# One transformer-style block on one core: the order of modulation's loads, and where splits and waits stand in five places

## The chip, the cores and the metric

The kernel runs on one core of a Trainium2 chip. The metric is the device time of one execution in microseconds (us), as the median over runs. The core's engines work side by side, each through its own list of instructions in order: TensorE (PE; its weight loads are PEld), VectorE (DVE), ScalarE (ACT), GpSimd (POOL) and SyncE (SP), which here issues the DMA transfers.

## The reference

One layer over 1024 latent tokens and 256 context tokens, width 1024, in float32. Cut to its core:

```python
mod_x = silu(c) @ w_ada + b_ada            # six vectors of 1024: shift, scale, gate, twice
mod_c = silu(c_ctx) @ w_ada + b_ada        # the same for the context tokens
px = modulate(rms_norm(x, g_pre_mix), sh_m, sc_m) @ w_in
pc = modulate(rms_norm(ctx, g_pre_mix), csh_m, csc_m) @ w_in
att_x = window_attention(...)              # 8 query heads, 2 key heads, band of 128, context keys, a sink
ml_x = mlstm_output(mlstm_bidir(...))      # chunkwise mLSTM in both directions, 4 heads
mix_x = concatenate([att_x, ml_x]) @ w_out
x = x + gt_m * rms_norm(mix_x, g_post_mix)
h = modulate(rms_norm(x, g_pre_ffn), sh_f, sc_f)
fx = (silu(gate) * up) @ w_ffn_out         # gate, up = split(h @ w_ffn_in), hidden 2816
x = x + gt_f * rms_norm(fx, g_post_ffn)
```

modulate(h, shift, scale) is h * (1 + scale) + shift.

## The kernel before

**Splits.** To keep float32's accuracy on TensorE, an operand is split into a high part (a cast to a shorter format, on ACT, `split` at L60) and a low part (the operand less the high part, on DVE at L61, on GpSimd in a few places), and a product is three matmuls, high by high, low by high and high by low (`mm3`, L72 to L74). [...]

**The modulation** (L265 to L320). Two of the six sections of `w_ada` are needed ahead of the input projection: `sec` 1 (scale), then `sec` 0 (shift). Each is eight tiles `wa` of 128x1024 (512 KB, L272), for the rows kt 0 to 7. The table `PLAIN` says which tiles are multiplied unsplit (`pr<-wa,cz`); the others are split into `hh` and `hl`. The results of a section (`pr`, 4x1024) are copied into `Vc`, half by ACT (L302) and half by DVE (L303), then transposed into columns (`pcol`, L309), which become `scol` (scale) and `hcol` (shift). All of this runs while weights arrive. `last` and `issue_after` chain the transfers into one order on SP: a transfer is issued behind the one named. Two more transfers stand there: `const` (masks, selections and the 128x128 identity, tile `cst`) and `bcv` (tile `bcr`), and the two pieces of the gate weights `w1` (`wr`, L260), each split into `w1h` and `w1l`.

**The first slabs.** Each of the ten tiles of 128 tokens is normalised, transposed and modulated: `prep_a` (load, squares on ACT, square root, and the scaling by GpSimd at L198; `prep_a2` at L183 for tile 2), `prep_t` (transposes on TensorE, L210), `prep_m` (eviction with the scale, L224), `prep_b` (adding `hcol`, L235; high parts, L244 and L247; low parts, L248). Then `slab` multiplies a tile by columns of `w_in`.

**Attention items.** Sixteen items (n, g), a tile of queries and a key head each. `PLAN_ML` (the first eight, which also carry the mLSTM) and `PLAN` (the rest) are strings whose letters order an item's operations: A scores, T transposes of the probabilities (L917), M the products with the values, N the normalising of the next item, O the output, z, V, s, x the mLSTM, l loads. An item's softmax runs on ACT (L898) and DVE (L889) two items ahead, and GpSimd scales the probabilities (L903). `WLOADS` says at which item `wout_load(j)` is called for each of the eight row tiles of `w_out`: it loads the raw tile (512 KB), casts it on ACT (L858) and subtracts on GpSimd (L859).

**Output projection and FFN.** `omm(n, hf, ks)` are the matmuls of tile n with `w_out`, `opost1` and `opost2` the norm and the residual, `otr` the transposes for the FFN (L1132), `omod` their modulation. The functions' calls around the last attention items and the first FFN products are written out by hand. ACT loads a table of functions when it turns from exponentials to square roots (L177). In the FFN, `xv` are PSUM tiles of the input product, evicted by ACT (L1282) or DVE; `es_add(0)` is a DVE addition for the first of them. A call to `keep_in_program_order` holds an instruction at its place in the program on its engine; other instructions are ordered by a list scheduler.

Of the kernel before, what the change touches and what calls it, by code (L numbers as in the profile page):

```python
# [29 lines left out]
CID, CUP, CLO, CSEL, CIND = 0, 128, 256, 384, 512  # L30
NCONST = 576
VSIL, VCONV, VGML, VBADA, VGPM, VGPF = 0, 16, 28, 32, 64, 72
NVEC = 80
PLAN_ML = "T0 A0 A1 A2 A3 T1 T2 T3 M0 M1 T4 V0 N0 M2 M3 M4 O z V1 w s N1 x"
PLAN = "T0 A0 A1 A2 A3 T1 T2 T3 N0 M0 T4 M1 M2 N1 M3 M4 O z l"
PLAN13 = "T0 A0 A1 A2 A3 m T1 T2 P0 T3 N0 M0 T4 M1 P1 M2 N1 M3 P2 M4 O P3 l"
WLOADS = {8: (0, 1), 9: (2,), 10: (3,), 11: (4,), 12: (5, 6), 13: (7,)}


def body(tc, x, ctx, vecs, bcv, bada, gqm, gqf, wada, ws1, ws2, wt, wout, wfi, wfo,  # L40
# [65 lines left out]
    ident = cst[:, CID:CID + P]  # L106
# [73 lines left out]
    def prep_a2(i):  # L180
        r = st[:, 10 + i:11 + i]
        tc.keep_in_program_order(dve.reciprocal(r, r))
        pool.tensor_scalar(xts[i], xts[i], r, 1.0, MUL, MUL)  # L183

    def prep_a(i, parts=(0, 1)):

        j = i - NT
        xt = xts[i] = R(4 + i % 4, f"xt{i}", (D,))
        xd[i] = dma(xt, x[i * P:(i + 1) * P] if i < NT else ctx[j * P:(j + 1) * P])
        hraw[i] = R((2, 3)[i] if i < 2 else (12, 13, 8, 9, 10, 11)[i % 6], f"hraw{i}", (KT, P))  # L190
        sq = act.activation(hraw[i].rearrange("p a b -> p (a b)"), xt, AF.Square, accum_out=st[:, i:i + 1])
        if i > 1:
            tc.keep_in_program_order(sq)
        if 1 not in parts:
            act.activation(st[:, 10 + i:11 + i], st[:, i:i + 1], AF.Sqrt, bias=epst, scale=1.0 / D)
            return
        rms_r(st[:, 10 + i:11 + i], st[:, i:i + 1])
        pool.tensor_scalar(xt, xt, st[:, 10 + i:11 + i], 1.0, MUL, MUL)  # L198
# [18 lines left out]
    def prep_m(i):  # L217
# [5 lines left out]
        for b in range(2):  # L223
            dve.tensor_tensor(raw2[i][b], pts[i][b], hcast(scol[:, i // NT, 4 * b:4 * b + 4]), MUL)  # L224

    def prep_b(i):
# [7 lines left out]
        for b in (1, 0) if i == 0 else range(2):  # L234
            r = (dve if i < 2 else pool).tensor_tensor(raws_[b], raws_[b], hcast(hcol[:, q, 4 * b:4 * b + 4]), ADD)  # L235
            if i == 1:
                tc.keep_in_program_order(r)
        if i == 0:
            prep_a2(2)
        for b in range(2):  # L240
# [7 lines left out]
            dve.tensor_tensor(ls[b][:, :, tok], raws_[b], h_.bitcast(F32), SUB)  # L248
# [9 lines left out]
    def w1_load(i):  # L258
        w1r[i] = R(i, f"wr1_{i}", (4, 272))
        r = dma(w1r[i], ws1[:, i])  # L260
        for k in (0, 2):
            split(w1h[i][:, k:k + 2], w1l[i][:, k:k + 2], w1r[i][:, k:k + 2])
        return r.ins

    PLAIN = {1: (0, 2, 4), 0: (0, 3, 7)}  # L265
    last, nsp = None, 0
    for sec in (1, 0):
        pr = [pa.tile([4, 512], F32, name=f"pr{sec}{i}", tag="mm", bufs=4) for i in range(2)]
        for kt in range(KT):
# [10 lines left out]
            for n, (a, b) in enumerate(ops):  # L280
                for i in range(2):
                    pe.matmul(pr[i], a[:, kt, :], b[:, i * 512:(i + 1) * 512], start=kt == 0,
                              stop=kt == KT - 1 and n == len(ops) - 1)
            if (sec, kt) == (1, 0):
                with tc.issue_after(last):
                    dma(cst, const)
                    last = dma(bcr, bcast(bcv)).ins
                dve.tensor_scalar(mF, up, -1.0, -NEG, ADD, MUL)
                dve.tensor_scalar(mB, lw, -1.0, -NEG, ADD, MUL)
            if (sec, kt) == (0, 1):  # L290
# [4 lines left out]
                prep_t(0)  # L295
            if (sec, kt) in ((0, 3), (0, 5)):
                with tc.issue_after(last):
                    last = w1_load(kt // 5)
        if sec == 0:
            prep_t(1, True)  # L300
        r4 = Vc.rearrange("p n h v -> p (n h v)")[0:4, 0:D]
        act.copy(r4[:, 0:512], pr[0])  # L302
        dve.tensor_copy(r4[:, 512:D], pr[1])  # L303
        if sec == 0:
            with tc.issue_after(last):
# [4 lines left out]
        for q in range(2):  # L310
# [5 lines left out]
            else:  # L316
                dve.tensor_tensor(t, pc_[:, :, q], bcol(0), ADD)
                dve.tensor_tensor(t, pc_[:, :, 2 + q], t, ADD)
# [57 lines left out]
    for n in range(2):  # L376
        prep_m(n)
    prep_b(0)
    prep_b(1)
    with tc.issue_after(xd[2].ins):  # L380
        prep_a(3)
    for i in range(NI):
# [305 lines left out]
    for j, name in enumerate(TILES):  # L688
# [45 lines left out]
        if name == "aq3":  # L734
# [7 lines left out]
            pool.tensor_scalar(nsk, nsk, -1.0, 1.0, MUL, MUL)  # L742
# [110 lines left out]

    def wout_load(j):
        h, l = R(2 * j, f"woh{j}", (D,), F32R), R(2 * j + 1, f"wol{j}", (D,), F32R)
        raw = R(2 * j + 2, f"wor{j}", (D,)) if j < 7 else V.rearrange("p n h v -> p (n h v)")[:, 0:D]
        dma(raw, wout[j])
        act.copy(h, raw)  # L858
        pool.tensor_tensor(l, raw, h.bitcast(F32), SUB)  # L859
        wo[j] = h, l  # L860
# [106 lines left out]
    for i in range(NIT):  # L967
# [4 lines left out]
        if i == NIT - 2:  # L972
            break
        for k in (PLAN_ML if i < NT else PLAN13 if i == NIT - 3 else PLAN).split():
# [21 lines left out]
            elif op == "l":  # L996
                for j in WLOADS[i]:
                    wout_load(j)
            elif op == "m":
# [27 lines left out]
    msplit(1, 1)  # L1027
    mm_t(b2, 0, 1)
# [205 lines left out]
    for n in range(1, NT):  # L1234
# [3 lines left out]
        else:  # L1238
            mixsplit(n, 0)
        opost1(n - 1)  # L1240
        if n > 1:
            mixsplit(n, 0)
# [13 lines left out]
        omm(n, 0, range(2))  # L1256
# [4 lines left out]
        omm(n, 0, range(2, 4))  # L1261
# [190 lines left out]
    omod(N1, True)  # L1452
    fi2(1)
# [21 lines left out]
    es_add(0)  # L1475
# [361 lines left out]
def pack(i):  # L1837
# [17 lines left out]
    def ttile(z):  # L1855
# [8 lines left out]
        + [a[k][0].reshape(KT, P).T for k in ("g_pre_mix", "g_pre_ffn")], 1)  # L1864
# [26 lines left out]
```

## Time and profile before

| | before |
|---|---|
| time, median of 3 runs | 1206.69 us (1205.56 to 1209.35) |
| the profiled execution's own time | 1208.04 us |
| its span | 1206.3 us |
| TensorE busy | 1175.6 us, 97% |
| VectorE busy | 819.1 us, 68% |
| ScalarE busy | 574.3 us, 48% |
| GpSimd busy | 155.2 us, 13% |
| mean granted TensorE clock | 0.996 |
| moved by DMA | 208.59 MB |

The profile describes one execution; its span runs from the first to the last instruction. "Busy" leaves out waiting. A row of the timeline gives the start and the length in us, the engine, the line of the program, the operation, output <- inputs with their shapes, the number of instructions, and in brackets how long the engine was idle ahead of it and who ended that. A row of the chain of waits gives start, length, and the engine and line on which the end depended then. A row of the windows gives the stretch, its length, the busy time of PE, PEld, DVE, ACT and POOL (with the number of instructions), then the granted clock (1.00 is full), the DMA share and GB/s.

### The profile page before, as it was taken

The page shows a single profiled execution, that of the slowest core. Times are in us where ns is not written, and L with a number is a line of the kernel's source. Part 1 is how long each engine was busy: PE and PEld are TensorE (multiplying, and loading weights), DVE is VectorE, ACT ScalarE, POOL GpSimd, SP SyncE. Part 2 cuts the span into 40 slices and gives each one's busy share as a digit, 9 for nine tenths or more (in the row PEclk, how much of TensorE's full clock was granted, in tenths as well). Part 3 has the DMA queues.
Part 4 walks back from the last instruction along what each step waited for, and adds up shares of the span by engine and source line. Part 5 has one row for each costly group of instructions (what it writes and reads, how often), then busy time and mean ns, then how long its engine had stood idle before and what let it go on. Part 6 is the DMA issues. An engine that isn't in the chain of part 4 may idle for free.

```text
span 1206.3 us, 16267 instructions
## 1 busy us (share of the span) xinstructions
PE 1175.6 (97%) x5859; PEld 964.7 (80%) x5859; DVE 819.1 (68%) x1436; ACT 574.3 (48%) x1066; POOL 155.2 (13%) x197
## 2 busy tenths in 40 slices
PE   6899999999999999999999999999999999999997
PEld 1699888877878778788788888888888888888886
DVE  5883768863888885457877677776777656554567
ACT  5653442222766795787634333333433335434443
POOL 1560001225433391000000000000000000000000
PEclk9999999999999999999999999999999999999999
DMA  9521964657745411431133556566644647665853
GB/s 352 185 86 44 365 213 150 200 144 233 178 136 144 129 36 36 178 102 69 62 123 131 181 213 226 181 221 236 217 162 134 202 156 267 205 214 186 306 189 126
DMA packets 100008, 208.59 MB, mean 173 GB/s; under 512 B 9684, under 2 KB 38740, under 8 KB 98520
## 3 DMA queue, kind: packets, MB, share of 16 engines
q1 hardware_dynamic: 99928, 207.56, 51.9%
q8 instruction: 46, 0.75, 0.3%
q14 instruction: 34, 0.28, 0.1%
HBM read 154.04 MB, written 52.83 MB: 171 GB/s over the span
## 4 chain that ended last, share of the span: by engine, by line
PE 88%; DVE 5%; ACT 4%; issue 1%; DMA 1%; POOL 0%; SPq 0%; DVEq 0%; ACTq 0%; POOLq 0%
PE xv L72 8%; PE xv L74 8%; PE xv L73 8%; PE pt L72 6%; PE pt L74 6%; PE pt L73 6%; PE t L551 4%; PE t L549 4%; PE t L548 4%; PE op L74 2%; PE op L73 2%; PE op L72 2%; PE fx L72 2%; PE slab L73 2%; PE fx L74 2%; PE slab L72 2%
## 5 line engine op out<-in xcount | busy, mean ns | idle before, releaser
L61 DVE TENSOR_TENSOR fo<-fr,fo 128x1024 fp32r<-128x1024 f32 x77 | 92.8, 1222 | 71.3 <-ACT fo L60 71.3
L60 ACT CAST fo<-fr 128x1024 fp32r<-128x1024 f32 x77 | 79.6, 1052 | 74.0 <-PE pt L74 38.1
L548 PE MATMUL t<-hh,th 128*128 128x512 f32 x208 | 82.4, 396 | 0.0
L549 PE MATMUL t<-hl,th 128*128 128x512 f32 x208 | 81.8, 393 | 0.0
L1306 ACT CAST wS<-wr 128x512 fp32r<-128x512 f32 x88 | 54.2, 622 | 55.8 <-PE pt L74 37.4
L1308 DVE TENSOR_TENSOR wS<-wr,wS 128x512 fp32r<-128x512 f32 x88 | 60.4, 689 | 20.7 <-ACT wS L1306 20.7
L72 PE MATMUL xv<-tT,wS 128*128 128x512 f32 x168 | 66.1, 394 | 0.0
L551 PE MATMUL t<-hh,tl 128*128 128x512 f32 x208 | 66.0, 395 | 0.0
L74 PE MATMUL xv<-tT,wS 128*128 128x512 f32 x168 | 65.7, 391 | 0.0
L73 PE MATMUL xv<-tT,wS 128*128 128x512 f32 x168 | 65.6, 391 | 0.0
L72 PE MATMUL op<-woh,mh 128*128 128x512 f32 x128 | 51.0, 398 | 0.0
L74 PE MATMUL op<-woh,ml 128*128 128x512 f32 x128 | 50.1, 391 | 0.0
L73 PE MATMUL op<-wol,mh 128*128 128x512 f32 x128 | 50.0, 391 | 0.0
L1058 DVE TENSOR_TENSOR wr<-wr 128x512 f32<-128x512 f32 x66 | 45.5, 689 | 1.4
L548 PEld LDWEIGHTS t<-hh,th 128*128 128x128 f32 x208 | 39.1, 188 | 8.3 <-issue 0.3
L1340 ACT ACTIVATE es<-es 128x512 f32<-128x512 f32 x22 | 13.9, 632 | 66.5 <-DVE es L1061 66.5
L549 PEld LDWEIGHTS t<-hl,th 128*128 128x128 f32 x208 | 39.2, 188 | 7.7 <-issue 0.7
L551 PEld LDWEIGHTS t<-hh,tl 128*128 128x128 f32 x208 | 37.5, 188 | 7.5 <-issue 1.4
L74 PE MATMUL pt<-fo 128*128 128x512 f32 x110 | 42.9, 390 | 0.0
L72 PE MATMUL pt<-fo 128*128 128x512 f32 x110 | 42.9, 390 | 0.0
L73 PE MATMUL pt<-fo 128*128 128x512 f32 x110 | 42.8, 389 | 0.0
L887 PE MATMUL s<-k,qh 128*128 128x256 f32 (+1 forms) x128 | 41.0, 330 | 1.2 <-DVE sm L889 1.1
(994 smaller groups left out, 3405.3 us busy)
## 6 DMA issues: line engine op xcount, KB each, us to landing
wr<-in_wfi SPq DMA_DIRECT2D x44, 512.0 KB, 5.3
wb<-in_wada SPq DMA_DIRECT2D x24, 512.0 KB, 6.2
s_d<-a SPq DMA_DIRECT2D x22, 512.0 KB, 6.7
bt<-in_wfo SPq DMA_DIRECT2D x44, 256.0 KB, 3.8
tb_d<-bt SPq DMA_DIRECT2D x11, 1024.0 KB, 3.9
fr<-s_d SPq DMA_DIRECT2D x44, 256.0 KB, 4.4
fr<-tb_d SPq DMA_DIRECT2D x44, 256.0 KB, 4.4
fr<-a_d SPq DMA_DIRECT2D x33, 256.0 KB, 4.6
```

The lines of the kernel that those rows point to most:

```text
L60: act.copy(hi, raw)
L61: dve.tensor_tensor(lo, raw, hi.bitcast(F32), SUB)
L72: pe.matmul(ps, a[0], b[0], start=first, stop=False, **kw)
L73: pe.matmul(ps, a[0], b[1], start=False, stop=False, **kw)
L74: pe.matmul(ps, a[1], b[0], start=False, stop=last, **kw)
L548: pe.matmul(o, wh[:, kt], m[0], start=f, stop=False)
L549: pe.matmul(o, wh[:, kt], m[1], start=False, stop=False)
L551: pe.matmul(o, wl[:, kt], m[0], start=False, stop=l)
L887: pe.matmul(o, qh[:, h, :], k2[g][:, kc], start=True, stop=False)
L1058: dve.tensor_tensor(out, a, b, SUB)
L1306: act.copy(w[:, 0], raw)
L1308: dve.tensor_tensor(w[:, 1], raw, w[:, 0].bitcast(F32), SUB)
```

## The change

Five places are changed. No product changes in value.

1. *Modulation and its loads.* The identity goes from `const` into `vec`, which is the first transfer; every transpose takes it from there (`ident`). `bcv` and `const` are loaded later: `bcv` behind the w1 pieces, `const` behind tile 3 of x; the masks `mF` and `mB` are computed in the slab loop. The two w1 pieces are loaded behind the last tile of section 0, and their splits are placed by hand (`w1_split`). Eleven matmuls of a tile of ones (`warm`) stand on TensorE ahead of the first weights. In section 0, tile 2 is plain in place of tile 3. Tile 3 is cast on ACT and subtracted on GpSimd, and its low matmuls stand behind the high ones of tile 4 (`low3`). Tile 6's low matmuls (`late`) stand behind tile 7's, and the transposes of token tile 1 stand ahead of tile 7's.
2. *First slabs.* Token tile 2 is scaled by ACT; tile 3's square root, reciprocal and scaling are placed by hand, as are several additions and splits.
3. *`w_out`.* In items 1 to 8 (plan letter p) a raw tile is split into one pair of buffers (`woxh`, `woxl`); the pair is stored to device memory (`wo_d`) at the next item, and loaded again in items 7 to 12. There is one raw buffer, so a raw tile is loaded behind the stores of the pair before it.
4. *Output projection.* ACT's table is loaded by an instruction of its own at the last attention items; all of `omm(1, 0, ...)` stands ahead of `otr(0)`; `mixsplit(1, 0)` stands behind `opost1(0)`.
5. *FFN start.* The second half of the first `xv` gets a PSUM tile of its own, and `es_add(0)` is called earlier.

```diff
-PLAN_ML = "T0 A0 A1 A2 A3 T1 T2 T3 M0 M1 T4 V0 N0 M2 M3 M4 O z V1 w s N1 x"
-PLAN = "T0 A0 A1 A2 A3 T1 T2 T3 N0 M0 T4 M1 M2 N1 M3 M4 O z l"
+PLAN_ML = "T0 A0 A1 A2 A3 T1 T2 T3 M0 M1 T4 V0 N0 M2 M3 M4 O z V1 w s N1 x p l"
+PLAN = "T0 A0 A1 A2 A3 T1 T2 T3 N0 M0 T4 M1 M2 N1 M3 M4 O z p l"
-WLOADS = {8: (0, 1), 9: (2,), 10: (3,), 11: (4,), 12: (5, 6), 13: (7,)}
+WLOADS = {7: (2,), 8: (0, 3), 9: (1, 4), 10: (5,), 11: (6,), 12: (7,), 13: ()}
...
-    ident = cst[:, CID:CID + P]
+    ident = vec[:, VID:VID + P]
...
     def prep_a2(i):
-        r = st[:, 10 + i:11 + i]
-        tc.keep_in_program_order(dve.reciprocal(r, r))
-        pool.tensor_scalar(xts[i], xts[i], r, 1.0, MUL, MUL)
+        tc.keep_in_program_order(act.activation(xts[i], xts[i], AF.Copy, scale=st[:, 10 + i:11 + i]))
...
-    PLAIN = {1: (0, 2, 4), 0: (0, 3, 7)}
+    PLAIN = {1: (0, 2, 4), 0: (0, 2, 7)}
+    last, nsp, late = None, 0, []
+    wm = pa.tile([P, 4, P], F32, name="warm", tag="tp", bufs=2)
+    for i in range(11):
+        pe.matmul(wm[:, i % 4], ones, ones, start=True, stop=True)
...
-                split(wh, wl, w)
+                if (sec, kt) == (0, 3):
+                    act.copy(wh, w)
+                    pool.tensor_tensor(wl, w, wh.bitcast(F32), SUB)
+                else:
+                    split(wh, wl, w)
...
+            if (sec, kt) == (0, 3):
+                low3 = ops.pop()
+            if (sec, kt) == (0, 4):
+                ops.insert(1, low3)
+            if (sec, kt) == (0, KT - 2):
+                late = ops[1:]
+                ops = ops[:1]
+            if (sec, kt) == (0, KT - 1):
+                ops += late
...
-            if (sec, kt) == (1, 0):
-                with tc.issue_after(last):
-                    dma(cst, const)
-                    last = dma(bcr, bcast(bcv)).ins
...
-            if (sec, kt) in ((0, 3), (0, 5)):
+            if (sec, kt) == (0, 7):
+                for i in range(2):
+                    with tc.issue_after(last):
+                        last = w1_load(i)
+                w1_split(0)
                 with tc.issue_after(last):
-                    last = w1_load(kt // 5)
+                    last = dma(bcr, bcast(bcv)).ins
+            if (sec, kt) == (0, 6):
+                prep_t(1, True)
+                prep_m(0)
+                prep_m(1)
...
+    def wout_raw(j):
+        if j:
+            for d, t in zip(wo_d, wraw.pop(j - 1)):
+                dma(d[j - 1], t.bitcast(F32))
+        if j < KT:
+            wraw[j] = qa.tile([P, D], F32, name=f"wor{j}", tag="wor", bufs=1)
+            with tc.issue_after(qlast[0]):
+                dma(wraw[j], wout[j])
+    def wout_split(j):
+        raw = wraw.pop(j)
+        h, l = (qa.tile([P, D], F32R, name=f"wox{p}{j}", tag=f"wox{p}", bufs=1) for p in "hl")
+        tc.keep_in_program_order(act.copy(h, raw))
+        tc.keep_in_program_order(pool.tensor_tensor(l, raw, h.bitcast(F32), SUB))
+        wraw[j] = h, l
     def wout_load(j):
-        dma(raw, wout[j])
-        act.copy(h, raw)
-        pool.tensor_tensor(l, raw, h.bitcast(F32), SUB)
-        wo[j] = h, l
+        wo[j] = tuple(R(2 * j + p, f"wo{'hl'[p]}{j}", (D,), F32R) for p in range(2))
+        for t, d in zip(wo[j], wo_d):
+            with tc.issue_after(qlast[0]):
+                dma(t.bitcast(F32), d[j])
...
     msplit(1, 1)
+    act.preload_act_table_set("sqrt_and_others")
...
-            xv[p] = [t[:, 0:512], t[:, 512:D]]
+            xv[p] = [t[:, 0:512], t[:, 512:D] if p else pb.tile([P, 512], F32, name="xv0b", tag="po", bufs=1)]
...
-        omm(n, 0, range(2))
+        if n == 1:
+            omm(n, 0, range(4))
+        else:
+            omm(n, 0, range(2))
...
     omod(N1, True)
+    es_add(0)
```

The first place is the end of the modulation. SP's transfers before (`wa` weight tiles, `xt` token tiles, `wr` the w1 pieces), from the third tile of section 0 on:

```order
L272 DMA wa_2_241<-in_wada 128x1024
L272 DMA wa_3_249<-in_wada 128x1024
L260 DMA wr_0_253<-in_ws 128x1088
L272 DMA wa_4_259<-in_wada 128x1024
L272 DMA wa_5_267<-in_wada 128x1024
L260 DMA wr_1_275<-in_ws 128x1088
L272 DMA wa_6_281<-in_wada 128x1024
L272 DMA wa_7_289<-in_wada 128x1024
L189 DMA xt_305<-in_x 128x1024
```

and now:

```order
L294 DMA wa_2_239<-in_wada 128x1024
L294 DMA wa_3_253<-in_wada 128x1024
L294 DMA wa_4_259<-in_wada 128x1024
L294 DMA wa_5_269<-in_wada 128x1024
L294 DMA wa_6_277<-in_wada 128x1024
L294 DMA wa_7_297<-in_wada 128x1024
L268 DMA wr_0_303<-in_ws 128x1088
L268 DMA wr_1_305<-in_ws 128x1088
L336 DMA bcr<-in_bcv 128x24
L188 DMA xt_317<-in_x 128x1024
L188 DMA xt_358<-in_x 128x1024
L424 DMA cst<-in_const 128x448
```

The w1 pieces have moved from between the weight tiles to behind them, and the constants stand behind a token tile.

TensorE there, before, with the last rows of section 0 (`hl_104` a low part, `pt` the transposes of token tile 1, `pcol` the columns):

```order
L282 MATMUL pr_203<-hh_102,cs_122 4x512
L282 MATMUL pr_204<-hh_102,cs_122 4x512
L282 MATMUL pr_203<-hl_104,cs_122 4x512
L282 MATMUL pr_204<-hl_104,cs_122 4x512
L282 MATMUL pr_203<-wa_7_289,cz_123 4x512
L282 MATMUL pr_204<-wa_7_289,cz_123 4x512
L210 MATMUL pt<-cst,xt_224 128x128 x8
L309 MATMUL pcol<-cst,Vc 128x4 x8
```

and now:

```order
L319 MATMUL pr_211<-hh_102,cs_122 4x512
L319 MATMUL pr_212<-hh_102,cs_122 4x512
L319 MATMUL pr_211<-hl_104,cs_122 4x512
L319 MATMUL pr_212<-hl_104,cs_122 4x512
L319 MATMUL pr_211<-hh_102,cs_122 4x512
L319 MATMUL pr_212<-hh_102,cs_122 4x512
L209 MATMUL pt<-vec,xt_232 128x128 x8
L319 MATMUL pr_211<-wa_7_297,cz_123 4x512
L319 MATMUL pr_212<-wa_7_297,cz_123 4x512
L319 MATMUL pr_211<-hl_104,cs_122 4x512
L319 MATMUL pr_212<-hl_104,cs_122 4x512
L352 MATMUL pcol<-vec,Vc 128x4 x8
```

The transposes of token tile 1 stand ahead of the plain tile 7, and tile 6's low matmuls behind it.

The second place is SP in attention items 8 and 9, now (`wor` a raw tile of w_out, `woxh` and `woxl` its parts on their way out, `woh` and `wol` reloaded, `qh` and `ql` queries); before, no stores or raw loads of this kind stood there:

```order
L911 DMA wo_dh<-woxh_4239 128x1024
L722 DMA qh<-aq_dh 64x4x128 x2
L722 DMA ql<-aq_dl 64x4x128
L911 DMA wo_dl<-woxl_4240 128x1024
L915 DMA wor_4259<-in_wout 128x1024
L928 DMA wol_4586<-wo_dl 128x1024
L722 DMA ql<-aq_dl 64x4x128
L928 DMA woh_4691<-wo_dh 128x1024
```

The last raw load stands behind the stores of the pair ahead of it. On ACT the last cast then stands between softmax steps of item 9 (L966) and casts of probabilities (L61):

```order
L61 CAST th__4455<-pt 128x512
L966 ACTIVATE pr__4483,sm<-pr__4483,sm 128x641
L61 CAST th__4498<-pt 128x512
L920 CAST woxh_4359<-wor_4259 128x1024
L966 ACTIVATE pr__4483,sm<-pr__4483,sm 128x641
L61 CAST th__4531<-pt 128x512
```

The third place is ACT at the start of the output projection, before (`t` the norm's working tile, `st` its statistics):

```order
L935 COPY o_5015<-po 64x512
L60 CAST mh<-mix 128x512
L1110 ACTIVATE t_5060,st<-op 128x1024
L177 ACT_TABLE_LOAD
L177 ACTIVATE st<-st,epst 128x1
L1118 ACTIVATE t_5060,st<-xt_5045 128x1024
L177 ACTIVATE st<-st,epst 128x1
L1120 ACTIVATE t_5060<-xt_5045,st 128x1024
```

and now:

```order
L61 CAST th__5022<-pt 128x512
L61 CAST mh_5026<-mix 128x512
L1100 ACT_TABLE_LOAD
L61 CAST th__5040<-pt 128x512
L1003 COPY o_5079<-po 64x512
L1183 ACTIVATE t_5120,st<-op 128x1024
L178 ACTIVATE st<-st,epst 128x1
L61 CAST mh<-mix 128x512
```

The table load has moved from behind L1110 to ahead of two operations of the attention.

More of the change, by code (lines that the diff above doesn't have):

```diff
@@ L259, in w1_load, with w1_split @@
         w1r[i] = R(i, f"wr1_{i}", (4, 272))
[L260 to L263, printed above, removed]
-    PLAIN = {1: (0, 2, 4), 0: (0, 3, 7)}
-    last, nsp = None, 0
+        return dma(w1r[i], ws1[:, i]).ins
+    def w1_split(i, part=None):
+        if part is None or -1 in part:
+            for k in (0, 2):
+                r = act.copy(w1h[i][:, k:k + 2], w1r[i][:, k:k + 2])
+                if part:
+                    tc.keep_in_program_order(r)
+        for k in (0, 1) if part is None else part if part[0] >= 0 else ():
+            sl = slice(2 * k, 2 * k + 2)
+            r = dve.tensor_tensor(w1l[i][:, sl], w1r[i][:, sl], w1h[i][:, sl].bitcast(F32), SUB)
+            if part:
+                tc.keep_in_program_order(r)
+    PLAIN = {1: (0, 2, 4), 0: (0, 2, 7)}
[3 more added lines that the diff above has]
+        pe.matmul(wm[:, i % 4], ones, ones, start=True, stop=True)
     for sec in (1, 0):
@@ L316, in body @@
             else:
[L317 to L318 removed]
+                for b in (bcol(0), t):
+                    tc.keep_in_program_order(dve.tensor_tensor(t, pc_[:, :, q if b is not t else 2 + q], b, ADD))
     pool.memset(Vc[:, :, :, 128:129], 1.0)
@@ L380, in body @@
     with tc.issue_after(xd[2].ins):
-        prep_a(3)
+        prep_a(3, (0,))
+    with tc.issue_after(xd[3].ins):
+        dma(cst, const)
     for i in range(NI):
@@ L852, in ml_out @@
         dve.tensor_tensor(mix[n][:, 4:8, :], pt, so, MUL)
-    def wout_load(j):
-        h, l = R(2 * j, f"woh{j}", (D,), F32R), R(2 * j + 1, f"wol{j}", (D,), F32R)
-        raw = R(2 * j + 2, f"wor{j}", (D,)) if j < 7 else V.rearrange("p n h v -> p (n h v)")[:, 0:D]
-        dma(raw, wout[j])
-        act.copy(h, raw)
-        pool.tensor_tensor(l, raw, h.bitcast(F32), SUB)
-        wo[j] = h, l
+    wo_d = [tc.dram_tile([KT, P, D], F32, name=f"wo_d{p}") for p in "hl"]
+    wraw = {}
+    def wout_raw(j):
[12 more added lines that the diff above has]
+        wraw[j] = h, l
+    def wout_load(j):
+        wo[j] = tuple(R(2 * j + p, f"wo{'hl'[p]}{j}", (D,), F32R) for p in range(2))
+        for t, d in zip(wo[j], wo_d):
+            with tc.issue_after(qlast[0]):
+                dma(t.bitcast(F32), d[j])
     def blocks(n):
@@ L996, in body @@
             elif op == "l":
-                for j in WLOADS[i]:
+                for j in WLOADS.get(i, ()):
                     wout_load(j)
+            elif op == "p" and 1 <= i <= KT:
+                wout_split(i - 1)
             elif op == "m":
@@ L1260, in body @@
         omod(n - 1, n == 7)
-        omm(n, 0, range(2, 4))
+        if n > 1:
+            omm(n, 0, range(2, 4))
         if n in (3, 4):
```

71 lines of the change are left out of this document (43 added, 28 removed).

## The prediction

> **What bounds the kernel now.** I read the page's first part, then the windows, the chain of waits by stage, and single rows of the timeline where a wait ends.
>
> ```profile
> PE 1175.6 (97%) x5859; PEld 964.7 (80%) x5859; DVE 819.1 (68%) x1436; ACT 574.3 (48%) x1066; POOL 155.2 (13%) x197
> ```
>
> TensorE is idle for 1206.3 - 1175.6 = 30.7 us. The change takes no matmul out of the products, so it can only earn idle time, or time in which the granted clock is low. The windows (busy us of PE, PEld, DVE, ACT, POOL, then the clock) say where both lie:
>
> ```profile
> 0.00:10.00 10.00, 3.66 (x5) 0.47 (x6) 0.83 (x5) 4.12 (x6) 1.04 (x11) 1.00 0.67 232
> 20.00:30.00 10.00, 6.90 (x33) 2.35 (x32) 8.35 (x17) 8.13 (x15) 2.23 (x2) 1.00 1.02 409
> 380.00:400.00 20.00, 19.77 (x130) 16.15 (x129) 16.98 (x52) 13.94 (x40) 7.08 (x10) 1.00 0.49 159
> 420.00:453.00 33.00, 29.41 (x183) 24.09 (x181) 29.53 (x66) 32.26 (x66) 29.07 (x28) 1.00 0.11 33
> 453.00:457.00 4.00, 3.71 (x13) 3.02 (x14) 3.94 (x9) 2.57 (x7) 2.21 (x2) 0.57 0.00 0
> 466.00:500.00 34.00, 32.45 (x163) 26.46 (x162) 16.46 (x24) 19.89 (x38) 0.00 (x0) 1.00 0.43 155
> ```
>
> Three stages hold what can be had: the modulation (6.3 and 3.1 us idle in two of its windows, the DMA share at 1.02), the last attention items (420 to 457, where ScalarE is busy 32.26 of 33 us), and the start of the output projection (1.55 us idle).
>
> **Part 1, loads and modulation.** The chain that ends it, and the landings:
>
> ```profile
> 28.14 1.05 ACT L60 CAST hh<-wa 128x1024 fp32r<-128x1024 f32 x1 [0.29 <-DMA wa<-in_wada]
> 29.44 1.20 ACT L60 CAST w1h<-wr 128x544 fp32r<-128x544 f32 x2 [0.25 <-DMA wr<-in_ws]
> wr<-in_ws SPq DMA_DIRECT2D x2, 544.0 KB, 10.3
> cst<-in_const SPq DMA_DIRECT2D x1, 288.0 KB, 4.8
> ```
> ```profile
> 31.01 1.36 DVE w1l L61 x2
> 32.37 1.15 DVE hl L61
> 33.56 2.45 PE pr L282 x6
> 36.03 0.68 DVE Vc L303
> 36.71 1.20 DVE hraw L224 x2
> 38.01 0.18 DVE hcol L318
> 38.21 0.47 ACT hh L244
> 38.72 3.73 PE slab L338 x16
> ```
>
> wa_5' lands at 28.1, the second w1 piece at 29.4, and 512 KB take 1.28 us at 409 GB/s, so wa_6' lands near 30.7 and wa_7' near 32.0. The change takes 2x544 + 288 + 12 KB (w1, const, bcv) from ahead of wa_7' and adds 64 KB (the identity): 1324 KB, 3.3 us. By that wa_7' lands at 28.7 and wa_2' to wa_6' at 22.3, 23.6, 24.9, 26.1 and 27.4. But the splits behind the loads don't all move by 3.3 us. Working forward in the new order: TensorE does wa_2' (1.88) and the transposes of tile 0 (1.09) to 25.3. Tile kt 3 is cast by 24.65, and then its low part goes to GpSimd, behind two scalings there (the L198 row below ends at 25.96; 0.6 earlier, 25.4), so 25.4 to 27.8. The low matmuls of kt 3 stand on TensorE behind kt 4's high part: 27.8. If DVE is undisturbed, the low parts of kt 4, 5 and 6 end at 27.2, 29.1 and 30.3; TensorE then does five pairs from 27.8 on (the 0.62 row below, overlapping, so about 0.47 from one to the next), eight transposes (1.09), wa_7' (1.9) and the last pair (0.5), to 33.6, against 36.0 now: 2.4 us.
>
> DVE is not undisturbed. Each of these rows is a DVE operation with both inputs in SBUF, beside a GpSimd operation or alone:
>
> ```profile
> 24.84 1.12 POOL L198 TENSOR_SCALAR xt<-xt,st 128x1024 f32<-128x1024 f32 x1 [0.46 <-DVE st L178]
> 39.75 1.63 POOL L183 TENSOR_SCALAR xt<-xt,st 128x1024 f32<-128x1024 f32 x1 [1.92 <-DVE st L182]
> 39.75 2.17 DVE L248 TENSOR_TENSOR hl<-hraw,hh 128x512 fp32r<-128x512 f32 x2
> 44.21 0.68 DVE L248 TENSOR_TENSOR hl<-hraw,hh 128x512 fp32r<-128x512 f32 x1
> 440.30 2.41 POOL L859 TENSOR_TENSOR wol<-wor,woh 128x1024 fp32r<-128x1024 f32 x1
> 442.12 1.15 DVE L61 TENSOR_TENSOR ml<-mix,mh 128x512 fp32r<-128x512 f32 x1
> ```
>
> The subtraction at 442.12 overlaps GpSimd's by 0.59 us (440.30 + 2.41 - 442.12) and takes 0.47 longer than the 0.68 of the same shape alone: about 0.8 of an overlap is lost. kt 4's low part would start at 25.95 and overlap kt 3's by 1.85, so it and everything behind it comes 1.5 us later: 35.1, a gain of 0.9. Behind the end, the change takes the tile-1 transposes and their two evictions (the 1.20 row) from ahead of the modulation columns, and puts one w1 split of 0.68 there; the columns' matmuls are then released by Vc at once, about 0.25 earlier. I take **1.2 us**; bounds 0 (the transposes now ahead of wa_7' wait for a scaling behind kt 3) and 2.6 (no overlap).
>
> [...]
>
> The eleven warm-up matmuls:
>
> ```profile
> 5.81 3.57 PE L282 MATMUL pr<-wa,cz 128*4 128x512 f32 x4 [5.81 <-DMA wa<-in_wada]
> 11.73 1.88 PE L282 MATMUL pr<-wa,cz 128*4 128x512 f32 x4
> 9.91 0.62 PE L282 MATMUL pr<-hh,cs 128*4 128x512 f32 x2 [0.52 <-ACT hh L60]
> ```
>
> The first tile runs at half the rate of the third, and they may mend that, 1.7 us. Yet the next pair waits for the cast of the second tile anyway (0.52), and what comes then goes by the landings. So 0 (bounds 0 and 0.3, part of the 0.52).
>
> **Part 2, the first slab.** Tile 2's scaling goes from GpSimd to ScalarE, and the order of additions and scalings on GpSimd is written out. The DVE splits beside L183 take 2.17 where two alone take 1.36: 0.8, of which I put **0.6** on the path. The stretch from 40.2 to 43.65, just there, runs at about half clock:
>
> ```profile
> 40.00:42.00 2.00, 2.00 (x9) 1.79 (x9) 2.00 (x3) 0.22 (x1) 1.38 (x1) 0.58 1.00 380
> ```
>
> If fuller occupation before it keeps the clock up, 1.7 us more; I don't count it, because TensorE still waits about 2 us for the columns (36.0 to 38.7). Bounds 0 and 2.3.
>
> **Part 3, w_out split in earlier attention items.** What leaves 415 to 457, and what it costs there:
>
> ```profile
> L858 ACT CAST woh<-wor x7: 1039/1048/1067, 415.3 to 445.2; 128x1024 fp32r<-128x1024 f32 x7
> L859 POOL TENSOR_TENSOR wol<-wor,woh x7: 2368/2402/2411, 416.6 to 446.6; 128x1024 fp32r<-128x1024 f32 x7
> PE pt L917 <- DVE tl__4668 L61: 1.5, 1, 1.5
> ```
>
> Seven of the eight casts lie in 420 to 453, and in the new order two (the seventh and eighth) still do: five casts, 5.2 us off ScalarE, the engine that is full there. The next bound is DVE, 29.53 of 33. Without the stretched 0.47 it has 29.06 us of work, and at 97% (my choice, a little under ScalarE's 98% now) needs 29.95: 3.05 us shorter. TensorE itself has 29.41 busy, so this would make it 98% busy, as in 380 to 400. The low clock of 453 to 457 follows on TensorE's longest waits (1.5 us here), costs 4 x 0.43 = 1.7 us, and may vanish with them: half, 0.8. Against it stands that the eighth raw tile is only loaded once the seventh's low part has been stored, and ScalarE, in order, would wait for it with the softmax exponentials queued behind: about 0.85 us, somewhat under one row of L859 less the cast that hides it (2.40 - 1.05 = 1.35). Sum **3.0 us**; bounds 1.0 (DVE ends every wait; two more us lost to the raw tile) and 5.5 (no low clock, no wait).
>
> The casts and subtractions go to 300 to 416. ScalarE has 6 of 20 us free there; eight stores of 1 MB and as many reloads meet a queue at 159 GB/s. I cost both at nothing: free ScalarE time hides the casts (8.4 us on the path if it did not), and each query load stands four items ahead of its use.
>
> **Part 4, output projection.**
>
> ```profile
> 484.26 1.28 ACT L177
> 491.63 1.09 PE L1132 MATMUL pt<-cst,t 128*128 128x128 f32 x8 [1.50 <-ACT t L1120]
> 493.43 0.23 PE op L72
> ```
>
> The table load stands in the chain to the transposes L1132, which wait 1.50 us. It moves some us earlier, where it stands beside the last attention matmuls, and twelve matmuls (12 x 0.23 = 2.7 us) go ahead of the transposes. Either covers the wait: **1.5** (1.0 to 1.9; the low end if the earlier load delays an attention cast).
>
> **Part 5, start of the FFN.** `PE xv L72 <- ACT es L1282` is a wait for a PSUM bank to be evicted:
>
> ```profile
> PE xv L72 <- ACT es L1282: 0.7, 1, 0.7
> ```
>
> A bank of its own removes it, while the addition es_add moves ahead of splits on DVE: **0.3** (0 to 0.7).
>
> **Sum.** 1.2 + 0.6 + 3.0 + 1.5 + 0.3 = 6.6 us. The profiled execution took 1208.04 (span 1206.3, and 1.74 around it), so it becomes 1201.4. It lay 1.35 above the median of the runs, 1206.69, which becomes 1200.1.
>
> **Rivals.**
>
> *B, the bound passes on to DVE or to the late raw tile.* Part 3 gives 1.0 and the start 0: 6.6 - 2.0 - 1.2 = 3.4, 1203.3. For it: DVE is at 89% now; the kt 3 subtraction starts only after two scalings. Against: the chain in 420 to 453 runs mostly over ScalarE.
>
> *C, both low-clock stretches go and GpSimd's split does not meet DVE's.* 6.6 + 1.4 + 1.7 + 2.5 = 12.2, 1194.5. For it: both stretches follow TensorE's waits; against: the waits for the columns stay.
>
> *D, the modulation does not do what it says.* kt 3's low part on GpSimd takes 2.4 where DVE takes 1.22, kt 4's waits behind it, and the low matmuls stand in order before kt 5's. If DVE also loses to the two scalings (2 x 1.12 x 0.8 = 1.8), the start loses 0.6 instead of gaining 1.2, at 1201.9: inside the forecast's own range.
>
> *E, slower: GpSimd's eight subtractions now run beside a full DVE.* 8 x 2.4 = 19.2 us go to 300 to 416, where DVE is busy 16.98 of 20 us. If those operations lost 0.8 of every overlap, 19.2 x 0.85 x 0.8 = 13 us, with TensorE 98% busy behind them: 1206.69 - 6.6 + 13 = 1213. It decides from 6.6 us, half of that. Against it:
>
> ```profile
> 434.70 2.41 POOL L859 TENSOR_TENSOR wol<-wor,woh 128x1024 fp32r<-128x1024 f32 x1 [1.73 <-ACT woh L858]
> 435.36 0.69 DVE L936 TENSOR_TENSOR mix<-po,o 64x512 f32<-64x512 f32 x1
> 436.08 0.89 DVE L889 CUSTOM_DVE_ANT_0 pr__4511<-s,mask,bcr 128x640 f32<-128x640 f32 x1
> L889 DVE CUSTOM_DVE_ANT_0 pr__3663<-s,mask,bcr 128x640 f32<-128x640 f32 x4 | 3.4, 881 | 0.5 <-PE s L888 0.5
> ```
>
> Beside GpSimd, operations with an input in PSUM (po, s) keep their 0.69 and 0.89, and nearly all of DVE's in 300 to 416 read PSUM too (the last row is one of the groups of that stretch, 881 ns each).
>
> **How the numbers follow.** Forecast (with D) 0.57, its own range 1197.5 to 1202.8; B 0.17, half of it within 0.3% (3.6 us); C 0.14; E 0.08, and 0.04 that gains of a few us are eaten by something unseen. Faster by over 0.3% (what a measurement here can tell from no change) means below 1203.1: 0.57 + 0.14 + 0.06 = 0.77; same 0.15; slower 0.08. The range, 1194.2 to 1205.2, holds most of C and all of B, and leaves out E.
>
> **What would show it.** Right: the first slab matmul at about 37.3 instead of 38.72; L1132 and the second xv without a wait; in 420 to 453 ScalarE below 95% and TensorE above 97%; PEclk 1.00 near 454. Wrong: the subtraction of kt 3 not beside a stretched DVE split (then more is won); ScalarE idle before the eighth w_out cast; DVE means in 300 to 416 above today's (E); a low clock that comes back elsewhere.

## The result, and the profile after

The changed kernel takes 1200.65 us (median of 6 runs, 1199.46 to 1202.52) against 1207.28 (6 runs, 1205.56 to 1209.35) for the kernel before. The ratio is 0.9941, with a 95% interval of 0.993 to 0.9952: about 7 us less. Five more runs of the unaltered changed kernel, in a later comparison, had a median of 1200.51. The profiled execution took 1200.47, with a span of 1198.7; against the span before that is 7.6 us, and this is the difference that can be divided by stage.

The first part of the page and the windows of the changed kernel:

```profile
PE 1177.0 (98%) x5881; PEld 967.4 (81%) x5881; DVE 816.3 (68%) x1435; ACT 575.0 (48%) x1067; POOL 155.7 (13%) x197
```
```profile
0.00:10.00 10.00, 8.62 (x32) 5.34 (x33) 1.58 (x3) 4.72 (x7) 0.84 (x10) 1.00 0.80 284
20.00:30.00 10.00, 7.53 (x32) 2.47 (x33) 7.78 (x14) 7.08 (x12) 4.63 (x3) 1.00 1.04 408
380.00:400.00 20.00, 19.78 (x132) 16.61 (x132) 16.31 (x53) 14.83 (x42) 10.33 (x11) 1.00 0.98 328
420.00:453.00 33.00, 32.01 (x209) 27.43 (x210) 32.07 (x73) 30.27 (x67) 18.39 (x23) 1.00 0.68 210
453.00:457.00 4.00, 4.00 (x19) 3.29 (x18) 2.41 (x7) 2.19 (x5) 2.73 (x4) 1.00 0.00 0
466.00:500.00 34.00, 32.30 (x156) 26.19 (x156) 14.74 (x22) 22.01 (x44) 0.00 (x0) 1.00 0.44 155
```

TensorE's idle time fell from 30.7 to 21.7 us, but part of that is the warm-up's own work, which counts as busy: the changed kernel without it has 25.9 us of idle time at about the same span (1198.8). The windows are fixed in time, so behind a gain they hold slightly later work. In 420 to 453 TensorE went from 29.41 to 32.01 busy, ScalarE fell from 32.26 to 30.27, and VectorE is now the full one, 32.07 of 33. In 466 to 500, however, TensorE's idle time is 1.70 us where it was 1.55: no idle time was won there.

To see where the 7.6 us came from, the same TensorE instructions are found in both timelines, and the distances between them compared (start times in us):

| landmark | before | changed | won on the way there |
|---|---|---|---|
| first slab matmul | 38.72 | 35.61 | 3.1 |
| first mLSTM gate transpose | 104.03 | 100.86 | 0.1 |
| last attention scores | 458.25 | 451.03 | 4.05 |
| last transposes for the FFN | 575.28 | 567.70 | 0.36 |
| end | 1206.3 | 1198.7 | 0.0 |

### The profile page after: what moved, and what is told of

Read it like the earlier page. It is cut to its first block, busy times and chain, and to the rows that moved or that the text cites. A ratio compares the mean times of both kernels' runs of the same rounds, so it can differ in the third digit from the quotient of the medians.

```text
span 1198.7 us, 16356 instructions
## 1 busy us (share of the span) xinstructions
PE 1177.0 (98%) x5881; PEld 967.4 (81%) x5881; DVE 816.3 (68%) x1435; ACT 575.0 (48%) x1067; POOL 155.7 (13%) x197
## 4 chain that ended last, share of the span: by engine, by line
PE 68%; DVE 4%; ACT 2%; issue 1%; DMA 0%; SPq 0%; POOL 0%; DVEq 0%; ACTq 0%
PE xv L75 8%; PE xv L73 8%; PE xv L74 8%; PE pt L75 6%; PE pt L74 6%; PE pt L73 6%; PE op L75 2%; PE op L73 2%; PE op L74 2%; PE fx L73 2%; PE fx L75 2%; PE fx L74 2%; PE pt L871 1%; PE pt L867 1%; PE pt L985 1%; PE fy L73 1%
## 5 line engine op out<-in xcount | busy, mean ns | idle before, releaser
L61 ACT CAST fo<-fr 128x1024 fp32r<-128x1024 f32 x77 | 79.6, 1051 | 74.0 <-PE pt L75 36.5
```

The lines of the kernel that those rows point to most:

```text
L61: act.copy(hi, raw)
```

## The experiments

All are the changed kernel with one part altered, except where said. The first eight were run once each, the last three five times. "Slab start" is the first slab matmul. Runs whose start is the same program as the changed kernel's, beside the 35.61 itself, gave a slab start of 35.89, 35.92, 35.81 and, where TensorE waited longer for the weights (1.1 us in all, against 0.5), 36.89. So a difference below about 0.4 us between two single profiles says nothing there, and one execution can lie 1.3 us off with the same program. In the stretch from the gate transposes to the last scores, the seven profiles with the same attention stage and the same wait at its first scores (below) lie between 350.17 and 351.91; the changed kernel's own, 350.17, is the shortest of them.

**Warm-up matmuls left out.**

```diff
-    wm = pa.tile([P, 4, P], F32, name="warm", tag="tp", bufs=2)
-    for i in range(11):
-        pe.matmul(wm[:, i % 4], ones, ones, start=True, stop=True)
```

> The changed kernel without the eleven warm-up matmuls and their PSUM tile. Theory: the warm-up earns nothing (the second tile's cast sets the pace), so the first slab matmul stays at 35.6 within 0.3 us although the first tile's four matmuls take about 3.6 instead of 2.05; and the tile is what costs at 295: being the first PSUM tile of the program it moves the banks of all others, so that the first attention scores share a bank with the last sigmoid input. Without it the 0.95 us wait of the scores for that sigmoid is gone, and the first scores start 3.1 us, not 2.1, ahead of the kernel before. Rival: the warm-up carries the start (first slab matmul about 1.5 us later), and the wait at 295 comes from TensorE's lead alone and stays.

**Warm-up matmuls kept, in other PSUM tiles.**

```diff
-    wm = pa.tile([P, 4, P], F32, name="warm", tag="tp", bufs=2)
+    wm = [pa.tile([P, 512], F32, name=f"warm{i}", tag="mm", bufs=4) for i in range(4)]
     for i in range(11):
-        pe.matmul(wm[:, i % 4], ones, ones, start=True, stop=True)
+        pe.matmul(wm[i % 4][:, 0:P], ones, ones, start=True, stop=True)
```

> The changed kernel with the warm-up matmuls kept, but written to four tiles of the ring of banks that the kernel before opened first, so that all banks lie as before. Theory (banks): the 0.95 us wait at the first scores goes, first slab matmul at 35.6 within 0.2, span about 1.0 us below 1198.7. Rival (lead alone): the wait stays, span 1198.7 within 0.4.

Measured: slab start 35.86 without and 36.05 with the matmuls in other tiles, spans 1198.8 and 1198.6. The timeline of the run without them, at the first weight tile and the second's cast:

```profile
5.38 3.57 PE L316 MATMUL pr<-wa,cz 128*4 128x512 f32 x4 [5.38 <-DMA wa<-in_wada]
6.59 1.04 ACT L61 CAST hh<-wa 128x1024 fp32r<-128x1024 f32 x1 [2.02 <-DMA wa<-in_wada]
8.88 0.66 PE L316 MATMUL pr<-hh,cs 128*4 128x512 f32 x2
```

The first tile is at half rate again (3.57, against 1.88 for the third), and the next pair starts at 8.88 where it started at 8.03, but the slab start doesn't move beyond the scatter. The warm-up does what it says, and earns nothing that these profiles can show.

The second thing in these two runs is a wait that the change had brought in, at the first attention scores. Changed kernel, then the run without warm-up:

```profile
294.48 1.09 ACT L775 ACTIVATE so<-t 128x512 f32<-128x512 f32 x2 [8.35 <-PE t L601]
295.61 0.39 PE L955 MATMUL s<-k,qh 128*128 128x256 f32 x1 [0.95 <-ACT so L775]
```
```profile
294.33 1.09 ACT L772 ACTIVATE so<-t 128x512 f32<-128x512 f32 x2 [9.51 <-PE t L598]
294.36 0.28 PE L952 MATMUL s<-k,qh 128*128 128x256 f32 x1
```

It is gone in both runs. TensorE's lead is not what makes it: with the slab start at 36.89 in two runs further down, one has the wait (no early table load) and one has not (constants early). Moving only the warm-up's PSUM tile removes it, so I infer that it goes by which earlier tile's place in PSUM the first scores take: in the changed kernel that of one which the last sigmoid still reads (to 295.57, and the scores start at 295.61). No view shows the places themselves, and the run with the constants early lacks the wait although its warm-up is unaltered, so the wait depends on more than the warm-up's tile. Neither span is 1 us shorter, as I had expected of the second; their slab starts were 0.25 and 0.44 later, and the end of the attention came where it came before. What the wait costs is taken up again with the last runs.

**Old order of the output matmuls.**

```diff
-        if n == 1:
-            omm(n, 0, range(4))
-        else:
-            omm(n, 0, range(2))
+        omm(n, 0, range(2))
...
-        if n > 1:
-            omm(n, 0, range(2, 4))
+        omm(n, 0, range(2, 4))
```

> The changed kernel with the old order of the second tile's output matmuls (half of them ahead of the first transposes, half behind), the early table load kept. Theory: the twelve matmuls were cover that was needed behind the transposes; put back, the transposes wait about 0.2 us (1.5 less the 1.28 of the table load) and the 1.5 us wait for the low part of the third tile's mix near 494 goes: span about 1.3 us shorter. Rival: the wait for the low part comes from the split that moved behind opost1(0), and stays at about 1.5: span about 0.2 longer.

Measured: span 1197.8, 0.9 us shorter; from the last scores to the last transposes 114.9 us, against 116.7 in the changed kernel and 117.0 before. Neither wait is there any more. First the changed kernel's chain of waits, then the timeline of the experiment:

```profile
486.24 0.45 PE pt L1205 x4
486.72 2.90 ACT mix L1214 x8
489.62 1.01 ACT t L1183 x2
490.66 0.30 ACT st L178
491.25 1.29 DVE t L1185
492.63 1.23 DVE xt L1134
493.85 0.61 DVE ml L62
494.51 0.50 PE op L75
```
```profile
484.25 1.03 PE L1205 MATMUL pt<-vec,t 128*128 128x128 f32 x8
484.89 2.90 ACT L1214 ACTIVATE mix<-pt,hfc,sfc 128x128 f32<-128x128 f32 x8 [0.40 <-PE pt L1205]
492.32 0.69 DVE L62 TENSOR_TENSOR ml<-mix,mh 128x512 fp32r<-128x512 f32 x1
```

From the start of the transposes (486.08) the changed kernel needs 8.4 us until the third tile's low part is there: ScalarE's eight evictions, the next norm behind them, the residual, and only then the split. TensorE has eight transposes and 26 matmuls to do in that time, 7.0 us, and waits 1.47. With twelve matmuls left behind the transposes it has 9.5 us of work (it takes up the low part at 493.75) against 8.76 needed (493.01 - 484.25), and doesn't wait. The matmuls moved ahead were the cover of the next wait; the early table load alone was enough for the first. The rival is out: the split still stands behind `opost1(0)` here, and the wait is gone.

**`w_out` split where it was split before.**

```diff
-PLAN_ML = "... s N1 x p l"
-PLAN = "... O z p l"
+PLAN_ML = "... s N1 x"
+PLAN = "... O z l"
-WLOADS = {7: (2,), 8: (0, 3), 9: (1, 4), 10: (5,), 11: (6,), 12: (7,), 13: ()}
+WLOADS = {8: (0, 1), 9: (2,), 10: (3,), 11: (4,), 12: (5, 6), 13: (7,)}
...
+        dma(raw, wout[j])
+        act.copy(h, raw)
+        pool.tensor_tensor(l, raw, h.bitcast(F32), SUB)
...
```

> The changed kernel with w_out split in items 8 to 13 as before and no stores or reloads; all else as changed. Theory: the lead over the kernel before at the last scores falls from 7.2 to 2.1 us (5.1 less), ScalarE is over 96% busy there again and a stretch of half clock comes back near 450; span about 5 us longer, near 1203.8. Rival: part of the 5.1 us came from the shift of the whole stage or of its banks; then 3 us or less come back, and no low clock.

Measured: span 1202.5, 3.8 us longer, and 353.97 us from the gate transposes to the last scores, against 354.22 before and 350.17 in the changed kernel. Its windows:

```profile
420.00:453.00 33.00, 29.13 (x182) 24.08 (x182) 29.45 (x64) 31.43 (x64) 30.35 (x28) 1.00 0.11 33
453.00:457.00 4.00, 4.00 (x31) 3.62 (x30) 3.75 (x11) 2.58 (x7) 1.37 (x2) 1.00 0.00 0
```

The idle time of TensorE is back (3.9 us). I had expected 5.1 us to come back, and the rival 3 or less: measured are 3.8 against the changed kernel's own profile, the shortest of the seven, and 2.1 against the longest. The low clock is not back (1.00), and yet the stage takes within 0.25 us what it took before with the low clock in it. That is two differences that cancel. This run has the wait at the first scores, which the kernel before has not: from the gate transposes to the first scores it takes 194.76 us, against 193.66 before. And behind the last long wait of the stage, the same TensorE instructions, without a pause, take longer in the kernel before, here first, than in this run:

```profile
453.29 1.11 PE L917 MATMUL pt<-cst,pr__4403 128*128 128x128 f32 x4 [1.48 <-DVE tl__4668 L61]
458.25 0.28 PE L888 MATMUL s<-k,ql 128*128 128x256 f32 x1
```
```profile
451.04 0.66 PE L967 MATMUL pt<-vec,pr__4415 128*128 128x128 f32 x4 [1.48 <-DVE tl__4680 L62]
454.77 0.28 PE L938 MATMUL s<-k,ql 128*128 128x256 f32 x1
```

From the first row to the last these are 4.96 us with the low clock in them, against 3.73 at full clock: the low clock cost the kernel before 1.2 us. The wait ahead of it is 1.48 in both, so neither this wait nor the place of the `w_out` splits brings the low clock by itself.

**Constants loaded early, w1 loaded early.**

```diff
+            if (sec, kt) == (1, 0):
+                with tc.issue_after(last):
+                    dma(cst, const)
+                    last = dma(bcr, bcast(bcv)).ins
...
-                with tc.issue_after(last):
-                    last = dma(bcr, bcast(bcv)).ins
...
-    with tc.issue_after(xd[3].ins):
-        dma(cst, const)
```

> The changed kernel with the constants and bcv transferred behind the first weight tile again (the identity stays in the first transfer, so 224 + 12 KB). Theory: these two small transfers cost far more than their 0.6 us of bytes, because SP spends 0.9 us on issuing them ahead of the second tile and the engines are not full then; the second tile's cast moves from 6.62 to about 8.6, and the first slab matmul from 35.6 to about 37.4. Rival (bytes only, as I predicted): 0.6 us at both places.

```diff
+            if (sec, kt) in ((0, 3), (0, 5)):
+                with tc.issue_after(last):
+                    last = w1_load(kt // 5)
             if (sec, kt) == (0, 7):
-                for i in range(2):
-                    with tc.issue_after(last):
-                        last = w1_load(i)
```

> The changed kernel with the two w1 pieces loaded between the last weight tiles again; their splits stay where the change put them. Theory: the last four tiles land up to 2.7 us later, and since the chain from landing to the end has little slack, the first slab matmul comes 1.5 to 2.5 us later, near 37.6. Rival: VectorE and the transposes set the end and the landings are hidden: 0.5 us or less later.

The constants: the second tile's cast moves from 6.62 to 8.64, by 2.0 us and not by the 0.6 of the bytes, and the slab start from 35.6 to 36.89, by 1.3. The 2.0 is clear; the 1.3 is no more than one run with the unaltered start showed (36.89 too). Timelines of the changed kernel and of the experiment:

```profile
6.62 1.04 ACT L61 CAST hh<-wa 128x1024 fp32r<-128x1024 f32 x1 [1.99 <-DMA wa<-in_wada]
```
```profile
8.64 1.04 ACT L61 CAST hh<-wa 128x1024 fp32r<-128x1024 f32 x1 [3.95 <-DMA wa<-in_wada]
```

In the kernel before, SP's timeline shows one source of that: the two issues stand between the first and the second weight tile.

```profile
1.18 0.42 SPq L272 DMA_DIRECT2D wa<-in_wada  x1
1.65 0.42 SPq L286 DMA_DIRECT2D cst<-in_const  x1
2.12 0.43 SPq L287 DMA_DIRECT2D bcr<-in_bcv  x1
2.59 1.60 SPq L272 DMA_DIRECT2D wa<-in_wada  x3
```

Two issues, 0.47 us from one to the next, are 0.9 us, and 236 KB at 409 GB/s are 0.6; how the 2.0 divides was not measured apart.

The w1 pieces: slab start 39.73, 4.1 us later, more than either theory said. But the run changes more than the landings: VectorE's w1 splits, not held in place, moved ahead of the weight splits with the loads, and one of them met the subtraction on GpSimd:

```profile
24.21 2.37 POOL L302 TENSOR_TENSOR hl<-wa,hh 128x1024 fp32r<-128x1024 f32 x1
24.52 2.63 DVE L279 TENSOR_TENSOR w1l<-wr,w1h 128x544 fp32r<-128x544 f32 x1 [1.49 <-ACT w1h L274]
```

So 4.1 is what the early loads cost together with that order, and the share of the landings alone stays open.

**Tile kt 3 on VectorE.**

```diff
-                if (sec, kt) == (0, 3):
-                    act.copy(wh, w)
-                    pool.tensor_tensor(wl, w, wh.bitcast(F32), SUB)
-                else:
-                    split(wh, wl, w)
+                split(wh, wl, w)
```

> The changed kernel with tile kt 3 of the shift section split on VectorE like the others, its low matmuls still behind kt 4's high ones. [...] Rival: GpSimd's part is what frees VectorE, and the first slab matmul comes 1.2 us later.

Measured: slab start 34.96, earlier by 0.65 where less than 0.5 either way was expected (VectorE's delay of about 1.0 us behind GpSimd against 1.23 for the split on VectorE), and a span of 1197.2. The rival, that GpSimd's part frees VectorE, is out. Most of that gain of 1.5 in the span is something else: the slab stage ran at full clock, and took 63.73 us to the gate transposes instead of 65.25. In a later run with the same program up to there (below) the clock was low again and the stage took 65.33. The window of 36 to 40 us, here and there:

```profile
36.00:40.00 4.00, 3.92 (x30) 3.48 (x28) 3.97 (x10) 3.06 (x5) 0.00 (x0) 1.00 0.24 90
```
```profile
36.00:40.00 4.00, 4.00 (x21) 3.74 (x20) 3.35 (x7) 3.06 (x6) 0.00 (x0) 0.65 0.26 100
```

**No early table load.**

```diff
-    act.preload_act_table_set("sqrt_and_others")
```

> The changed kernel without the early table load. Theory: the load of 1.28 us falls back into the chain of opost1(0); the transposes of the first tile don't wait (twelve matmuls, 2.7 us, cover it), but everything behind them on ScalarE and VectorE is 1.28 later, and so the wait for the third tile's low part grows from 1.5 to about 2.7: span 1.2 us longer. Rival: ScalarE catches up under the twelve matmuls: the wait stays at 1.5, span unchanged within 0.3.

Measured: from the last scores to the last transposes 117.34 us, 0.7 more than in the changed kernel; the waits for low parts grow from 1.5 in one place to 2.4 in two. That is between the two expectations. The span, 1200.8, doesn't decide, since the slab start of this run is 1.3 us late, where the weights came late.

**Two parts undone, and the warm-up left out too.** The first kernel joins the edits of the tile-kt-3 run and of the run with the old matmul order; the second leaves the warm-up out as well; the third is the changed kernel unaltered.

> The changed kernel with two of its parts undone: tile kt 3 split on VectorE, and half of the second tile's output matmuls behind the first transposes. Theory (the two gains, 1.5 and 1.8 us in single profiles, lie in different stages and add): median 3.3 us below the changed kernel's 1200.65, near 1197.4; first slab matmul near 35.0, no wait of 1.5 at the output projection. Rival (the slab gain was a chance of where the clock's boundary fell): the output part alone, near 1199.

> As the run before, without the warm-up matmuls too. Theory (warm-up worth nothing, and the wait of the first scores that it causes is absorbed later): the same median within 0.5 us, although the first scores start 1 us earlier. Rival: the warm-up carries part of the start, 1 us or more slower.

> The changed kernel itself, unaltered, beside the two runs before on the same chip: a second sample of its start and of its time. Median within 1 us of 1200.65; first slab matmul between 35.6 and 36.1, as in the runs whose start is the same program; if it lies outside, differences below that spread between single profiles tell nothing.

| kernel | median us (5 runs) | ratio to the kernel before, 95% | slab start | gate transposes | last scores | last transposes |
|---|---|---|---|---|---|---|
| two parts undone | 1199.59 | 0.9942 (0.9928 to 0.9956) | 35.21 | 100.54 | 451.25 | 566.17 |
| and no warm-up | 1198.64 | 0.993 (0.9918 to 0.9943) | 35.62 | 100.67 | 450.02 | 564.98 |
| changed, again | 1200.51 | 0.995 (0.9935 to 0.9964) | 35.81 | 100.68 | 451.10 | 567.77 |

The first rival was right: undoing the two parts gives a median 0.9 us below the unaltered kernel's beside it, not 3.3, and the runs of the two overlap. The output part is 1.7 us in the traces each time (114.92 and 114.96 against 116.67 from the last scores to the last transposes); VectorE instead of GpSimd brings the slab start forward by 0.2 to 0.7 and the gate transposes by 0.1.

Without the warm-up the stretch from the gate transposes to the last scores is 1.4 us shorter (349.35 against 350.71). Divided at the first scores, all profiles of these kernels settle what the wait for the sigmoid costs. Up to them, the stretch takes 194.75 or 194.76 us in each of the eight profiles with the wait, and 193.64 to 193.66 in each of the five without it, the kernel before among them. Behind them, the profiles with `w_out` split early don't differ by it: 155.4 to 157.2 in the seven with the wait, 155.7 to 156.7 in the four without. So the wait costs 1.1 us up to there, and nothing shows that it is made good later; the expectation that it is absorbed is not borne out. The scatter behind the first scores, up to 1.7 us, hid this in the spans of the first two experiments. In time, the intervals of the first two kernels of the table overlap. The kernel with the two parts undone and no warm-up has the lowest median measured here, 1198.64.

## Why the prediction was right, and where it was not

The time was inside the range and near the sum: 6.6 us predicted, 7.6 between the two profiled executions; 1200.1 forecast, 1200.65 measured. The terms were not each right: parts 1, 3 and 5 gave more than they were priced at, and parts 2 and 4 gave next to nothing. That these errors nearly cancel is luck.

*Part 1, 1.2 us; measured about 3 (2.7 to 3.1, and 1.8 with the one late start).* The step that was mis-sized is the working from bytes to landings. Of its 3.3 us, 0.6 stand for the constants at the start, where the second tile came 2.2 us earlier (8.81 to 6.62). It counted their bytes at the full rate, not SP's two issues between the first tiles, nor that the engines were not full there (a DMA share of 0.67 in the first window, 0.80 after). kt 3 was cast at 22.72 instead of the 23.6 I worked from, and the three casts behind it came 0.8 to 0.9 earlier than worked out. The delay of VectorE was as worked out in kind, and smaller, 1.0 for 1.5. These two are about 1.4 of the 1.9 us by which the start came earlier than forecast; the rest was not traced. The changed kernel's timeline:

```profile
22.66 1.12 POOL L197 TENSOR_SCALAR xt<-xt,st 128x1024 f32<-128x1024 f32 x1 [0.46 <-DVE st L179]
23.85 2.39 POOL L302 TENSOR_TENSOR hl<-wa,hh 128x1024 fp32r<-128x1024 f32 x1
25.08 2.25 DVE L62 TENSOR_TENSOR hl<-wa,hh 128x1024 fp32r<-128x1024 f32 x1 [0.42 <-ACT hh L61]
26.30 0.62 PE L319 MATMUL pr<-hl,cs 128*4 128x512 f32 x2 [0.58 <-POOL hl L302]
```

kt 4's subtraction overlaps GpSimd's by 1.16 us (26.24 - 25.08) and takes 1.03 longer than its 1.22: 0.89 of the overlap, where I took 0.8. In the w1 experiment the overlap is 2.06 (26.58 - 24.52), and the split takes 2.63 where its like alone takes 0.72: 1.9 of it, or 0.93, against the 0.8 (0.47 of 0.59) of the row before the change. Splitting kt 3 on VectorE starts the slab 0.2 to 0.7 earlier, so this piece of part 1 took away from the gain.

*The warm-up, 0.* Right in its price. One of its two reasons no longer held: with the second tile 2.2 us earlier, the next pair waits for TensorE and not for the cast (without the warm-up it starts at 8.88, and the cast ends at 7.63). The other did: what comes later goes by the landings.

*Part 2, 0.6; measured 0.1.* The stretch from the slab start to the gate transposes took 65.31 before and 65.25 after (64.7 to 65.3 in all runs with the low clock there). The two splits do take 1.29 us now instead of 2.17, but the half clock is still there (0.50 in 38 to 40 us) and TensorE is what that stage waits for; taking 0.8 off VectorE took little or nothing off the path. What was on the path is the clock: 1.6 us between two runs of the same program (63.73 and 65.33). I had named that price, 1.7, and rightly not counted it.

*Part 3, 3.0; measured 4.05 between the two profiles.* The experiments divide this into three: 3.8 from the splits (2.1 to 3.8 with the scatter), 1.2 from the low clock that is gone, and 1.1 lost to the wait at the first scores. For the splits the mechanism, ScalarE full with casts and VectorE the next bound, was right, and VectorE filled to 97% (32.07 of 33), as assumed; the 3.05 us that I took for it lies within this. The 0.85 us for the late eighth raw tile was not lost, ScalarE never being idle ahead of a cast. The 0.8 for the low clock was half of a price of 1.7 that measured 1.2. It came, but not by the reason given: the run with the old splits has the same waits (0.50 and 1.48) and full clock, so why the clock was low in the kernel before, and whether the change is what removed it, stays open. The wait at the first scores was not foreseen at all.

*Part 4, 1.5; measured none.* This is the step that failed. From the last scores to the last transposes 0.36 us were won, and part 5's wait of 0.7 lay in that stretch, so part 4 by itself lost about 0.3. "Either covers the wait" was true of the transposes L1132, and the wait there is gone; but I did not ask what the twelve matmuls had covered where they stood. They stood between the transposes and the third tile's low part, and the same 1.5 us came back there, 8.4 us behind the start of the transposes. The early table load, which the experiment shows to be enough alone, also costs 0.2 where it stands, ahead of a cast of the attention: a wait of 0.23 for a low part at 474.82, which is absent in the run without the load.

*Part 5, 0.3; measured about 0.7.* The wait of 0.7 is gone: TensorE is busy 119.97 us of the 120 from 500 to 620. No run undoes this part alone.

*The rivals.* B's bound came (VectorE is full) without its price. C came in half: the low clock at 453 is gone (0.57 before, 1.00 now), the one in the slab stage stayed (0.50 in 38 to 40 us), and GpSimd's split did meet VectorE's. D's stall was there, 0.6 us of waiting for GpSimd, inside a start that gained anyway. E is refuted at its place. A group of scores in 300 to 416, in the changed kernel:

```profile
L957 DVE CUSTOM_DVE_ANT_0 pr__3523<-s,mask,bcr 128x640 f32<-128x640 f32 x4 | 3.4, 881 | 0.5 <-PE s L956 0.5
```

881 ns each, as before. One of the four starts at 351.86, inside a subtraction of `w_out` on GpSimd (351.79 to 354.16), and takes 0.88: these operations, which read PSUM, are not stretched here.

## What to carry to other kernels

Matmuls that are moved to cover one wait leave the place where they covered another: before moving them, work out the chain from there to the next thing that TensorE needs (here 8.4 us against 7.0 us of work left). Small transfers between the first large ones can cost far more than their bytes (here 2.0 us at the next tile for 0.6 us of bytes). A scratch tile in PSUM can change the waits much later: here one of 1.1 us, 290 us further on, came with it. Before a part is called worth nothing because two runs agree, divide the runs at landmarks: a loss and a gain of 1 us each had cancelled here.

## What the runs showed of the hardware that was not expected

The granted clock in the slab stage depends on more than the program: the same start ran 36 to 40 us at 1.00 in one execution and at 0.65 in another, after almost the same idle pieces of TensorE (0.44 us ahead of the columns' matmuls and 0.99 ahead of the first slab matmul in both). In the changed kernel, behind gaps of 0.43 and 0.99 us, it was 0.50 in 38 to 40 us. What decides between the two was not shown, and whether it is the sum of the gaps was not tried.

Half clock cost 1.6 us in the slab stage (65.33 against 63.73) and 1.2 us at 453 in the kernel before (4.96 against 3.73), where ScalarE and VectorE were the fuller engines over the whole window (32.26 and 29.53 us of 33 in 420 to 453, TensorE 29.41) but TensorE had work without a pause just then (453.29 to 458.25): in these two cases the price went by which engine set the pace in those few microseconds, not by the average of the stage.
